# One more lane step in the memory attention of a hybrid encoder layer, and higher pacing rates for its lane in five stages

## Chip, cores and metric

The kernel runs on one core of one Trainium2 chip. The metric is the device time of one execution in microseconds; lower is better. The core has five engines with queues of their own, which work side by side: TensorE (PE; its weight loads are listed apart as PEld), VectorE (DVE), ScalarE (ACT), GpSimd (POOL) and SyncE (SP), whose queue issues nearly all DMAs here.

## What is computed

One layer of a bidirectional encoder with three parallel groups of heads, on two requests (256 and 1024 tokens, together 10 tiles of 128) with shared weights, in float32:

```python
hn = rms_norm(x, norm_g)
xbc, z_ssd, dt_raw, q, k, v, z_att, mq, z_mem = split_cols(hn @ w_in, IN_SIZES)
...                                                    # o_ssd: convolution, state scan both ways, gate, norm
...                                                    # o_att: windowed attention with 8 heads, gate
memn = rms_norm(mem, mem_norm_g)
mk, mv = split_cols(memn @ w_mem_kv, (MEM_WIDTH, MEM_WIDTH))      # 256 memory rows, 4 heads of 128
sm = einsum('bthd,bmhd->bhtm', rms_norm(mq), rms_norm(mk)) * MEM_HEAD_DIM ** -0.5
pm = softmax(sm, axis=-1)
o_mem = einsum('bhtm,bmhd->bthd', pm, mv) * silu(z_mem)
return x + concatenate([o_ssd, o_att, o_mem]) @ w_out
```

## The kernel before

Two kinds of work are woven together.

**The blocks** are the large products with `w_in`, `w_mem_kv` and `w_out`. A block takes its weights tile by tile over the inner dimension (16 tiles `k` of 128). Each weight tile is loaded by DMA into `wraw` and split by ScalarE and VectorE (L206, L207) into a high part `wh` and a low part `wl`; three matmuls then make one float32 product (L258 to L260 in `block_tok`, which makes rows of 5 token tiles at a time, 15 matmuls a tile `k`; L293 to L295 in `block_feat`). Blocks come in a fixed order. After the first half of the tokens (group 0) the second half (group 1) takes the stages `kv`, `q`, `za`, `z0`, `z1`, `mq`, `zm`; then come the output blocks: four token blocks (`o`) and eight others over the whole output.

**The lanes** hold everything that isn't a block: normalising keys (`k_prep`), windowed attention (`attn`), memory attention (`mem_attn`) in lane 0; the step sizes (`dt_prep`) and the state scan up and down (`ssd_up`, `ssd_down`) in lane 1. Each is a Python generator for one token tile `t`, and its code from one `yield` to the next is one *lane step*. Steps are traced between the matmuls of the blocks: after each tile `k` the block calls `pump`, which credits each lane with that stage's rate and runs as many steps of it as there are whole credits, in turn with the other lane:

```python
for i in range(2):
    owed[i] = owed[i] + rates[i] if lanes[i] else 0.0
while max(owed) >= 1:
    i = turn[0] ^ 1
    i = turn[0] = i if owed[i] >= 1 else i ^ 1
    owed[i] -= 1
    if lanes[i]:
        step(lanes[i])
```

`RATES[1]` holds the pair of rates of each stage of group 1, lane 0 first. `block_feat` stages (`x`, `za`, `zm`) have two blocks or more of 16 calls at half the rate. In a token block the matmuls of the last two tiles `k` stand together, and their two calls come behind them, next to each other. What is needed before it has been traced is forced by `need`; what the lanes still hold in the third output block is emptied in one go there, and the pool `mp` is closed.

A planner in the framework turns this trace into the engines' queues: it takes instructions by priority and by the times at which it expects their data, so their order on an engine is near the order of the trace but not the same. Semaphores keep what depends on each other in order.

`mem_attn` handles a token tile in two pairs of heads. Step by step: load the queries; squares and norms; queries split, gates `zm` loaded; an empty step; `scores(0)`; `scores(1)`; an empty step; `turn_(0)`; `turn_(1)`; `values(0)`; `values(1)` and the store. `scores` makes the scores of a pair (TensorE, L745 to L747, into `pms`), takes their maximum (VectorE, L749, L750), the exponential with its sum (ScalarE, L754), and scales by the reciprocal of the sum (VectorE, L756, L759, into `mpr`). `turn_` transposes the probabilities on TensorE (L767, into `pmt`) and copies them out on ScalarE (L771, `mpT`). `values` multiplies by the memory's values (L782) and the gate (L785, `moT`). Tiles t = 0 to 4 come up from the end of stage `x` on, in `kv` and `q`; t = 5 to 9 in the first two output blocks.

Of the other lines that the prediction names, L641 and L643 are scores of windowed attention and their maximum, L625 its turned queries; L868 and L889 belong to the scan upwards, L1045 and L1062 to the scan downwards; L1009 and L1011 turn a finished tile of it; L213 loads a weight tile.

Of the kernel before, what the change touches and what calls it, by code (L numbers as in the profile page):

```python
# [29 lines left out]
RBB = 4  # L30

RATES = ({'kv': (4.0, 1.0), 'z1': (2.2, 1.7)},
         {'kv': (1.4, 1.5), 'x': (2.1, 2.15), 'q': (2.2, 2.5), 'za': (2.1, 2.5), 'z0': (2.1, 2.5),
          'z1': (2.05, 2.55), 'mq': (1.95, 2.7), 'zm': (1.75, 2.75), 'o': (2.1, 2.4)})
FAR = 1e30

UNITS = (0, 8, 1, 9, 2, 10, 3, 11, 4, 12, 5, 13, 6, 7)
# [7 lines left out]
def hymba_encoder_kernel(  # L45
# [37 lines left out]
    def psum(name):  # L83
        return mix.tile([P, 512], F32, tag="mix", name=name)
# [37 lines left out]
    def rsqrt(dst, src, scale, n):  # L122
        G.tensor_scalar(out=dst, in0=src, scalar1=scale, scalar2=EPS, op0=ALU.mult, op1=ALU.add)
        G.tensor_tensor(out=dst, in0=dst, in1=mhalf[:, :n], op=ALU.pow)

    def hv(ap, n=8):
        return ap.rearrange("p (h d) -> p h d", h=n)
# [287 lines left out]
    def w2(name):  # L415
        return mp.tile([P, 512], F32, tag="wa", name=name, bufs=WA)
# [286 lines left out]
    def mem_attn(t):  # L703
        grp, ti = divmod(t, 5)
        tc_ = slice(ti * P, (ti + 1) * P)
        qr = mp.tile([P, 512], F32R, tag="wa", name="mq", bufs=WA)
        q = qr.bitcast(F32)
        if grp == 0:
            S.dma_start(hv(q, 4), mT_d[:, :, tc_])
        else:  # L710
            S.dma_start(q, mq_d[t])
        yield

        def turned():
            ps = psum("pmq")
            for h in range(4):
                T.transpose(ps[:, h * P:(h + 1) * P].bitcast(F32R), qr[:, h * P:(h + 1) * P], identr)
            return ps

        tok_ = turned() if grp == 0 else q  # L720
        sq = w2("sq")
        A.activation(sq, tok_, AF.Square)
        ss = sm.tile([P, 4], F32, tag="s4", name="mss", bufs=4)
        V.reduce_sum(out=ss, in_=hv(sq, 4), axis=AX.X)
        r = sm.tile([P, 4], F32, tag="s4", name="mr", bufs=4)
        rsqrt(r, ss, 1.0 / P, 4)
        yield
        feat_ = q if grp == 0 else turned()
        qh = mp.tile([P, 512], F32R, tag="qT", name="mqh", bufs=2)
        A.activation(qh, feat_, AF.Copy)  # L730
        ql = mp.tile([P, 512], F32R, tag="qT", name="mql", bufs=2)
        V.tensor_sub(ql, feat_, qh.bitcast(F32))
        z = w2("zm")
        S.dma_start(hv(z, 4), zT_d[1][grp][:, :, tc_])
        yield
        yield
        st_ = {}

        def scores(hp):
            ps = psum("pms")  # L740
            for j in range(2):
                h = 2 * hp + j
                c = slice(h * P, (h + 1) * P)
                o = ps[:, j * 256:(j + 1) * 256]
                T.matmul(o, qh[:, c], mkH[:, h, :], start=True, stop=False)  # L745
                T.matmul(o, qh[:, c], mkL[:, h, :], start=False, stop=False)
                T.matmul(o, ql[:, c], mkH[:, h, :], start=False, stop=True)  # L747
            m = sm.tile([P, 2], F32, tag="m2", name="mm", bufs=10)
            V.reduce_max(out=m, in_=hv(ps, 2), axis=AX.X)  # L749
            V.scalar_tensor_tensor(out=m, in0=m, scalar=-1.0, in1=r[:, 2 * hp:2 * hp + 2], op0=ALU.mult, op1=ALU.mult)  # L750
            pr = mp.tile([P, 512], F32, tag="lg", name="mpr", bufs=2)
            den = sm.tile([P, 2], F32, tag="m2", name="mden", bufs=10)
            for j in range(2):
                A.activation(pr[:, j * 256:(j + 1) * 256], ps[:, j * 256:(j + 1) * 256], AF.Exp,  # L754
                             scale=r[:, 2 * hp + j:2 * hp + j + 1], bias=m[:, j:j + 1], accum_out=den[:, j:j + 1])
            V.reciprocal(out=den, in_=den)  # L756
            for j in range(2):
                c = slice(j * 256, (j + 1) * 256)
                V.tensor_scalar(out=pr[:, c], in0=pr[:, c], scalar1=den[:, j:j + 1], scalar2=0.5,  # L759
                                op0=ALU.mult, op1=ALU.mult)  # L760
            st_[hp] = pr

        def turn_(hp):
            pr = st_[hp]
            pt = psum("pmt")
            for a in range(4):
                T.transpose(pt[:, a * P:(a + 1) * P], pr[:, a * P:(a + 1) * P], ident)  # L767
            if hp == 0:
                st_["pT"] = mp.tile([P, 2, 768], F32, tag="pT", name="mpT", bufs=1)
            pT = st_["pT"][:, hp, :512]  # L770
            A.activation(pT, pt, AF.Copy)  # L771
            st_[hp] = pT

        oT = w2("moT")

        def values(hp):
            pT = st_.pop(hp)
            po = psum("pmo")
            for j in range(2):
                h = 2 * hp + j  # L780
                for a in range(2):
                    T.matmul(po[:, j * P:(j + 1) * P], mv[:, a, h * P:(h + 1) * P],  # L782
                             pT[:, (2 * j + a) * P:(2 * j + a + 1) * P], start=(a == 0), stop=(a == 1))
            c = slice(hp * 256, (hp + 1) * 256)
            V.tensor_mul(oT[:, c], po[:, :256], z[:, c])  # L785

        scores(0)
        yield
        scores(1)
        yield  # L790
        yield
        turn_(0)
        yield
        turn_(1)
        yield
        values(0)
        yield
        values(1)
        S.dma_start(oT_d[1][grp][:, :, tc_], hv(oT, 4))
        yield  # L800
# [649 lines left out]
    def refill_o(grp, when):  # L1450
        def f(k):
            if k not in when:
                return []
            q = when[k]
            need((attn, mem_attn, ssd_down, ssd_down)[q], range(grp * 5, grp * 5 + 5))
            return [part(fill_direct, q, j, oT_d[q][grp][:, j, :],
                         gain=None if q < 2 else vec[:, R_SG + 4 * (q - 2) + j:R_SG + 4 * (q - 2) + j + 1])
                    for j in range(4)]
        return f
# [126 lines left out]
    def when_done(n, then):  # L1586
# [9 lines left out]
        return f  # L1596

    queue(0, mem_attn, range(5))
    run(block_tok(w_in_rows("z1"), 5, ev_gate(1, 0)), RATES[0]["z1"], refill_x(1),
        extra=when_done(1, lambda: queue(1, ssd_up, range(4))))  # L1600
# [25 lines left out]
    tok("mq", w_in_rows("mq"), ev_raw(mq_d, 5), grp=1)  # L1626
    gate("zm", 1, refill_o(0, {3: 0, 7: 1}))
    queue(0, mem_attn, range(5, 8))
    queue(0, mem_swap, [0])
    queue(0, mem_values, [1])  # L1630
# [97 lines left out]
```

## Time and profile before

| what | value |
|---|---|
| time, median of 3 runs | 1793.29 us (1792.8 to 1793.42) |
| the profiled execution | 1792.72 us, of which the span from first to last instruction is 1791.0 us |
| granted clock of TensorE | 1.000 |
| PE, DVE, ACT, POOL busy | 99%, 70%, 51%, 31% of the span |
| DMA | 301.12 MB, mean 168 GB/s |

Line numbers (L767) are those of the kernel before. In the profile's rows `pmt<-identr,mpr` reads: tile `pmt` is written from `identr` and `mpr`; `128x512 f32` is partitions by elements. In a timeline the first two columns are the start and the duration in us, and `[1.09 <-DVE mpr L759]` says that the engine stood idle for 1.09 us before the instruction until that other instruction had ended. In a list of waits the three numbers are total us, count and the longest. A table by windows shows the busy time of each engine in each stretch of the span, with the number of its instructions.

### The profile page before, as it was taken

What the parts mean: (1) busy time and instruction counts of PE and PEld (TensorE: products, weight loads), DVE (VectorE), ACT (ScalarE), POOL (GpSimd) and SP (SyncE); (2) the same over time, 40 slices, a digit from 0 to 9 for tenths busy, and PEclk for the clock granted to TensorE, in tenths of its full rate; (3) what the DMA queues carried; (4) which work ended last, traced back from release to release, by engine and by line L of the source; (5) the groups of instructions that cost most, each with busy time, mean ns of one, the idle gap of its engine ahead of it and who ended that gap; (6) DMA issues with size and microseconds to landing.
All of it is one profiled execution on the core that took longest, in us unless ns stands there. A gap on an engine that the chain in (4) does not pass through costs nothing.

```text
span 1791.0 us, 31429 instructions
## 1 busy us (share of the span) xinstructions
PE 1777.5 (99%) x10838; PEld 1605.0 (90%) x10838; DVE 1248.7 (70%) x2358; ACT 922.2 (51%) x2049; POOL 549.6 (31%) x900
## 2 busy tenths in 40 slices
PE   9999999999999999999999999999999999999999
PEld 7789999999998999999889977877988888899999
DVE  5595788888868877778766575557777644766665
ACT  6554555554434766656465565544447533543332
POOL 0105789998810101001001000000100000057775
PEclk9999999999999999999999999999999999999999
DMA  8653444445446644453635645557777754744442
GB/s 292 199 180 114 144 148 149 144 142 163 123 145 207 188 142 137 136 162 111 193 111 179 182 149 162 165 160 249 233 224 238 240 185 149 223 149 144 148 142 77
DMA packets 208207, 301.12 MB, mean 168 GB/s; under 512 B 19568, under 2 KB 86192, under 8 KB 208048
## 3 DMA queue, kind: packets, MB, share of 16 engines
q1 hardware_dynamic: 207904, 299.06, 54.3%
q8 instruction: 85, 1.39, 0.3%
q14 instruction: 74, 0.61, 0.1%
q10 hardware_dynamic: 144, 0.06, 0.0%
HBM read 236.36 MB, written 62.69 MB: 167 GB/s over the span
## 4 chain that ended last, share of the span: by engine, by line
PE 71%; issue 7%; POOL 7%; DVE 6%; DMA 6%; ACT 3%; SPq 0%; POOLq 0%; ACTq 0%; DVEq 0%
PE acc L258 8%; PE acc L260 8%; PE acc L259 8%; PE acc L293 5%; PE acc L1237 5%; PE acc L295 5%; PE acc L294 5%; PE acc L1235 5%; PE acc L1236 5%; POOL ws L1207 4%; PE accm L1236 2%; PE accm L1235 2%; PE accm L1237 2%; POOL wraw L1207 2%; PE po L673 1%
## 5 line engine op out<-in xcount | busy, mean ns | idle before, releaser
L207 DVE TENSOR_TENSOR wl<-wraw,wh 128x512 fp32r<-128x512 f32 (+1 forms) x480 | 345.3, 721 | 220.0 <-ACT wh L206 199.8
L206 ACT ACTIVATE wh<-wraw 128x512 fp32r<-128x512 f32 (+1 forms) x480 | 292.1, 613 | 305.8 <-PE acc L260 154.1
L258 PE MATMUL acc<-wh,xH 128*128 128x512 f32 (+1 forms) x1088 | 418.4, 385 | 0.5 <-ACT mkr L420 0.3
L260 PE MATMUL acc<-wh,xL 128*128 128x512 f32 (+1 forms) x1088 | 411.2, 378 | 0.0
L259 PE MATMUL acc<-wl,xH 128*128 128x512 f32 (+1 forms) x1088 | 410.4, 377 | 0.7 <-DVE wl L207 0.7
L258 PEld LDWEIGHTS acc<-wh,xH 128*128 128x128 f32 x1088 | 204.5, 188 | 38.7 <-issue 3.6
L259 PEld LDWEIGHTS acc<-wl,xH 128*128 128x128 f32 x1088 | 204.6, 188 | 38.2 <-DVE wl L207 3.3
L260 PEld LDWEIGHTS acc<-wh,xL 128*128 128x128 f32 x1088 | 204.4, 188 | 36.8 <-issue 0.6
L293 PE MATMUL acc<-xH,wh 128*128 128x320 f32 x640 | 202.9, 317 | 0.5 <-DVE zs L309 0.5
L206 ACT ACTIVATE sh<-ws 128x384 fp32r<-128x384 f32 x176 | 91.4, 523 | 214.0 <-POOL ws L1207 117.0
L294 PE MATMUL acc<-xL,wh 128*128 128x320 f32 x640 | 199.2, 311 | 0.0
L295 PE MATMUL acc<-xH,wl 128*128 128x320 f32 x640 | 198.3, 310 | 0.0
L207 DVE TENSOR_TENSOR sl<-ws,sh 128x384 fp32r<-128x384 f32 x176 | 124.1, 708 | 105.1 <-ACT sh L206 104.9
L1207 POOL TENSOR_TENSOR ws<-wraw 128x128 f32<-128x128 f32 x176 | 113.5, 645 | 204.5 <-DMA wraw<-in_w_in_pairs_dram 81.1
L635 POOL COPY lg<-nsink 128x2 f32<-128x2 f32 x40 | 16.4, 410 | 373.9 <-PE ppt L663 239.6
L293 PEld LDWEIGHTS acc<-xH,wh 128*128 128x128 f32 x640 | 120.3, 188 | 3.3 <-issue 2.2
L294 PEld LDWEIGHTS acc<-xL,wh 128*128 128x128 f32 x640 | 120.3, 188 | 2.0 <-issue 1.7
L295 PEld LDWEIGHTS acc<-xH,wl 128*128 128x128 f32 x640 | 120.2, 188 | 0.8 <-issue 0.7
L1207 POOL TENSOR_TENSOR ws<-wraw,ws 128x128 f32<-128x128 f32 x176 | 116.6, 662 | 13.8
L1207 POOL TENSOR_TENSOR wraw<-wraw 128x128 f32<-128x128 f32 x176 | 112.2, 638 | 13.7
L1207 POOL TENSOR_TENSOR ws<-ws,wraw 128x128 f32<-128x128 f32 x176 | 115.0, 653 | 0.0
L362 DVE SCALAR_TENSOR_TENSOR c<-u,vec,c 128x638 f32<-128x638 f32 (+1 forms) x96 | 89.7, 936 | 8.9 <-ACT c L357 8.6
(437 smaller groups left out, 3947.0 us busy)
## 6 DMA issues: line engine op xcount, KB each, us to landing
wraw<-in_w_in_laid_dram SPq DMA_DIRECT2D x176, 256.0 KB, 2.9
wraw<-in_w_in_pairs_dram SPq DMA_DIRECT2D x112, 256.0 KB, 2.7
wraw<-in_w_out_laid_dram SPq DMA_DIRECT2D x64, 256.0 KB, 3.0
wraw<-in_w_out_pairs_dram SPq DMA_DIRECT2D x64, 256.0 KB, 2.9
rf<-ac SPq DMA_DIRECT2D x40, 256.0 KB, 4.0
rb<-ac SPq DMA_DIRECT2D x40, 256.0 KB, 4.9
wraw<-in_w_mem_laid_dram SPq DMA_DIRECT2D x32, 256.0 KB, 4.8
xst<-in_x_sample_dram SPq DMA_DIRECT2D x20, 256.0 KB, 4.9
```

Source lines behind the costliest of these rows:

```text
L206: a = A.activation(h, raw, AF.Copy)
L207: b = V.tensor_sub(l, raw, h.bitcast(F32))
L258: T.matmul(ps[t][:, :n], sh, h[:, :n], start=(k_ == 0), stop=False)
L259: T.matmul(ps[t][:, :n], sh, l[:, :n], start=False, stop=False)
L260: T.matmul(ps[t][:, :n], sl, h[:, :n], start=False, stop=(k_ == KT - 1))
L293: T.matmul(o, sh, cur["H", q][:, m, c], start=(k == 0), stop=False)
L294: T.matmul(o, sh, cur["L", q][:, m, c], start=False, stop=False)
L295: T.matmul(o, sl, cur["H", q][:, m, c], start=False, stop=(k == KT - 1))
L1207: G.tensor_tensor(out=o, in0=x, in1=y, op=op)
L1235: T.matmul(ps[p], h, xh, start=(k_ == 0), stop=False)
L1236: T.matmul(ps[p], h, xl, start=False, stop=False)
L1237: T.matmul(ps[p], l, xh, start=False, stop=(k_ == 7))
```

## The change

`mem_attn` yields once more between `scores(1)` and `turn_(0)`: two empty steps lie there instead of one, and each of its ten runs takes 13 lane steps instead of 12. In group 1 the rate of lane 0 is raised in the stages `kv` (1.4 to 1.5), `q` (2.2 to 2.25), `za` (2.1 to 2.15), `z1` (2.05 to 2.1) and `mq` (1.95 to 2.0), and in the output stage `o` (2.1 to 2.15). Lane 1's rates, and the rates of `x`, `z0` and `zm`, are as before.

```diff
-         {'kv': (1.4, 1.5), 'x': (2.1, 2.15), 'q': (2.2, 2.5), 'za': (2.1, 2.5), 'z0': (2.1, 2.5),
-          'z1': (2.05, 2.55), 'mq': (1.95, 2.7), 'zm': (1.75, 2.75), 'o': (2.1, 2.4)})
+         {'kv': (1.5, 1.5), 'x': (2.1, 2.15), 'q': (2.25, 2.5), 'za': (2.15, 2.5), 'z0': (2.1, 2.5),
+          'z1': (2.1, 2.55), 'mq': (2.0, 2.7), 'zm': (1.75, 2.75), 'o': (2.15, 2.4)})
...
         scores(0)
         yield
         scores(1)
+        yield
         yield
         yield
         turn_(0)
```

## The prediction

> **What bounds the kernel now.** The page comes first: its engine shares.
>
> ```profile
> span 1791.0 us, 31429 instructions
> PE 1777.5 (99%) x10838; PEld 1605.0 (90%) x10838; DVE 1248.7 (70%) x2358; ACT 922.2 (51%) x2049; POOL 549.6 (31%) x900
> ```
>
> TensorE (PE) has an instruction in flight in 99% of the span; the other engines have room. So the time is TensorE's own work plus the moments in which it stands still, and those are 1791.0 − 1777.5 = 13.5 us in all. The change adds, removes and reshapes no matmul: it can only move waits. The question is therefore which of these 13.5 us lie where the change reaches. The table by windows says so; I cut the span at 820 us (where memory attention begins), at 1480 us (where its last block has ended) and at 1591 us (where the last output blocks begin).
>
> ```profile
> core 0: us, PE busy (x) PEld busy (x) DVE busy (x) ACT busy (x) POOL busy (x), PEclk, DMA share, GB/s
> 0.00:820.00 820.00, 815.40 (x5143) 761.29 (x5144) 618.80 (x1116) 442.54 (x948) 342.25 (x541) 1.00 0.52 160
> 820.00:1480.00 660.00, 654.68 (x3858) 556.43 (x3857) 431.14 (x925) 357.11 (x885) 56.12 (x97) 1.00 0.61 189
> 1480.00:1591.00 111.00, 111.00 (x503) 91.13 (x503) 69.66 (x120) 48.13 (x85) 11.11 (x23) 1.00 0.54 167
> 1591.00:1791.00 200.00, 196.37 (x1339) 196.11 (x1337) 129.06 (x200) 74.38 (x134) 140.13 (x240) 1.00 0.44 134
> ```
>
> Everything before 820 us runs at rates and with steps that the diff leaves alone, and after 1480 us memory attention is over. Between them TensorE idles 660 − 654.68 = 5.3 us. That is what the change can work on. The list of TensorE's waits in this stretch gives 4.7 us of it a name:
>
> ```profile
> engine line waited for: us in total, times, longest us
> PE pmt L767 <- DVE mpr L759: 2.0, 3, 1.1
> PE pyb L1062 <- ACT so L1011: 1.1, 1, 1.1
> PE psc L641 <- DVE nm L643: 0.9, 1, 0.9
> PE pd L1045 <- DVE nm L643: 0.3, 1, 0.3
> PE psc L641 <- ACT qT L625: 0.2, 1, 0.2
> PE pst L868 <- DVE fl L889: 0.2, 1, 0.2
> ```
>
> The largest row is exactly the place of the new step: the turn of the probabilities (L767) waits for VectorE's scaling of them (L759), 2.0 us over three waits. The other 2.7 us belong to window attention (L641) and to the state scan (L868, L1045, L1062).
>
> **What one such wait costs, and why it is there.** The timeline at the worst one, the second memory attention block (t = 1, in the kv stage):
>
> ```profile
> 847.70 0.28 PE L747 MATMUL pms<-mkH,mql 128*128 128x256 f32 x1
> 851.10 0.56 ACT L754 ACTIVATE mpr<-pms,mm,mr 128x256 f32<-128x256 f32 x1 [0.55 <-DVE mm L750]
> 852.35 0.29 PE L260 MATMUL acc<-wh,xL 128*128 128x288 f32 x1
> 852.48 0.29 PE L258 MATMUL acc<-wh,xH 128*128 128x288 f32 x1
> 853.37 0.61 DVE L759 TENSOR_SCALAR mpr<-mpr,mden 128x256 f32<-128x256 f32 x2
> 853.86 0.52 PE L767 MATMUL pmt<-identr,mpr 128*128 128x128 f32 x3 [1.09 <-DVE mpr L759]
> ```
>
> The first pair's scores leave TensorE at 847.98 and the scaled probabilities are there at 853.37 + 0.61 = 853.98: a chain of 6.0 us over VectorE and ScalarE. TensorE reaches the turn after about 5 us. Its matmuls here start 0.13 us apart (852.35, 852.48), but from 852.48 to 853.86 it is 1.38 us: the wait costs 1.25 us, 0.16 more than the 1.09 in brackets. I count from start to start below. The other waits at L767, in blocks t = 6 and t = 7 (output stage):
>
> ```profile
> 1370.35 0.28 PE L747 MATMUL pms<-mkH,mql 128*128 128x256 f32 x1
> 1370.47 0.39 PE L258 MATMUL acc<-wh,xH 128*128 128x512 f32 x1
> 1370.70 0.39 PE L259 MATMUL acc<-wl,xH 128*128 128x512 f32 x1
> 1374.12 0.39 PE L259 MATMUL acc<-wl,xH 128*128 128x512 f32 x1
> 1375.30 0.63 PE L767 MATMUL pmt<-identr,mpr 128*128 128x128 f32 x4 [0.79 <-DVE mpr L759]
> 1375.69 0.48 PE L260 MATMUL acc<-wh,xL 128*128 128x512 f32 x1
> 1376.31 0.63 PE L767 MATMUL pmt<-identr,mpr 128*128 128x128 f32 x4
> 1402.30 0.60 PE L767 MATMUL pmt<-identr,mpr 128*128 128x128 f32 x4
> 1405.93 0.39 PE L260 MATMUL acc<-wh,xL 128*128 128x512 f32 x1
> 1406.47 0.30 PE L767 MATMUL pmt<-identr,mpr 128*128 128x128 f32 x1 [0.15 <-DVE mpr L759]
> ```
>
> Start to start against the undisturbed 0.23 us (1370.47 to 1370.70): 1375.30 − 1374.12 − 0.23 = 0.95; 1376.31 − 1375.69 − 0.23 = 0.39; 1406.47 − 1405.93 − 0.23 = 0.31. With the 1.25 the four waits cost 2.9 us.
>
> **The new step, counted out.** Four stages by the same table (kv, q, z0, first output block; I read their bounds off the evacuations of the blocks):
>
> ```profile
> 820.00:868.00 48.00, 46.87 (x365) 45.10 (x365) 38.45 (x86) 34.27 (x93) 5.47 (x5) 1.00 0.55 160
> 868.00:945.00 77.00, 76.94 (x414) 64.21 (x411) 51.98 (x120) 42.57 (x110) 5.43 (x10) 1.00 0.49 147
> 1011.00:1089.00 78.00, 77.00 (x407) 61.95 (x406) 48.79 (x110) 45.12 (x113) 4.39 (x9) 1.00 0.50 153
> 1328.00:1402.00 74.00, 72.86 (x400) 60.63 (x399) 47.22 (x93) 42.14 (x100) 3.84 (x7) 1.00 0.76 236
> ```
>
> A memory attention block takes 12 lane steps now and 13 after. The step issues no instruction. It only sets the turn later, so I counted the steps of both lanes call by call, with the old rates and the new ones (a call of the pacing stands behind each input tile of a block, 16 to a block; the last two calls of a token block stand next to each other). What matters is how many calls lie between a block's scores and its turns:
> - t = 1: scores in calls 8 and 9 of kv, turns in 10 and 11; after, both turns in 11. The first turn moves by a call, and 48 us of kv over 16 calls is 3.0 us a call (820 to 868): more than the 1.25 missing. That wait goes.
> - t = 6: both scores in call 8 of the first output block, both turns in 9; after, in 10. 74 us (1328 to 1402) over 16 calls is 4.6 us, against 0.95 + 0.39. Both waits go.
> - t = 7: scores in 13 and 14, turns in 15. After, the lane is later by then: both scores in 14, both turns in call 0 of the next block. Between them lies the k = 0 group of that block, 15 matmuls, 3.4 us: the pattern that t = 6 has before. So a new wait may stand there. Its bounds: nothing (block t = 3 has the same pattern in the q stage, where TensorE idles for 0.06 us in all, 77.00 − 76.94), or t = 6's 1.34. I take 1.3, since it is the same stage and load.
> - The others have two calls or more, or the distance they had.
>
> Sum: − 2.9 + 1.3 = − 1.6 us.
>
> **The rates.** Five memory attention blocks add 5 steps before zm. The raised rates give back 16 × 0.1 in kv, 16 × 0.05 in q, 32 × 0.025 in za, 16 × 0.05 in z1 and in mq: 4.8 steps. Window attention t = 4 to 9 and the key preparation in front of it so start in the same call as before or up to three calls later (three only inside za), and the last one ends in the same call of zm. In the output stage 41 calls × 0.05 give 2.05 against 5 steps: the lane ends two calls later, with seven calls left before what remains of the lanes is emptied. Lane 1 keeps its rates and its calls. So no step is forced, and no pool closes later.
>
> What is queued with a step: each block's loads of its queries and gates and its store go to SP's queue, in front of weight loads.
>
> ```profile
> SPq L213 <- DVE moT L785: 18.5, 7, 5.1
> ```
>
> Weight loads already stand behind the block's last product for up to 5.1 us, and no wait of the weight matmuls is in TensorE's list for this stretch: the loads run ahead. I cost this at nothing; without that lead a late load would cost up to those 5.1 us. The two buffers of probabilities are held one step longer, and the next user comes at least five steps behind the turn: nothing.
>
> The other 2.7 us of listed waits are re-dealt, since attention shifts by up to a call (4.6 us in the output stage, 78 / 16 = 4.9 in z0) against the state scan. They can vanish (− 2.7, with 0.16 a wait − 3.5) or be joined by others; without a row that favours a side I take zero and keep both ends for the range.
>
> The profiled execution took 1792.72 us (span 1791.0 and 1.7 around it), 0.57 under the median 1793.29. After: 1791.1 by the profile, **1791.7** by the median. About 0.2% (3.6 us) is what a measurement of this kernel can tell from no change.
>
> The matmul row's 99% caps any gain at the 5.3 us. The Trainium skill (Perfetto Trace Analysis, "Identifying the Most-Contended Engine") calls matmul busy time no good measure of headroom and takes LDWEIGHTS busy time instead; by that, 820 to 1480 us would hold 660 − 556.43 = 104 us. The trace speaks against using it here: from 1480 to 1591 us TensorE never idles (111.00 of 111) and its loads are busy for 91.13, 82%, about the 84% of our stretch. So its result changes nothing in my sum.
>
> **The rivals.**
> 1. *The planner undoes it.* TensorE's order is not the program's order alone: in block t = 7 both turns come out of one call, yet stand at 1402.30 and 1406.47, with 15 matmuls between. If turns stand where the planner expects their data, a step changes little, and the waits stay: 1793.3. Against it: t = 1 and t = 6 stand one call behind their scores, as counted.
> 2. *The shift helps attention too.* The 3.5 us above go and the new wait of t = 7 does not come: 1791.7 − 4.8 = 1786.9; about half of it gives 1789. It is over 0.2% from 2.0 of these 4.8 on. For it: these waits are single accidents of place. Against it: all must fall well.
> 3. *Slower: attention and state scan collide.* Lane 0 is denser in q, za, z1 and mq while lane 1 stays. Both use VectorE and ScalarE in order, and TensorE's transposes and state products (L641, L1009, L1045, L1062) stand in its queue ahead of the weight matmuls. A call's shift may set one directly behind its producer, at the price of L1062's or L641's wait: 1.1 or 0.9, with 0.16 more each. It decides from + 3.6 + 1.6 = 5.2 us on, that is five new waits; five or six give 1797.5 to 1798.5. For it: six blocks of attention and ten of state work lie in reach, each with several such points. Against it: the stretch has only five such waits now.
>
> **How the numbers follow.** My forecast 0.36 and the planner 0.14 both lie within 0.2%: same 0.50. Rival 2: faster 0.24. Rival 3: slower 0.26. The likeliest case alone runs from 1790 (no new wait at t = 7) to 1794 (two new ones elsewhere). The range reaches from 1787.5, short of rival 2's end, to 1799, past six collisions.
>
> **What would show it.** Right: L767 has no wait in kv; one or two near the seam between the first two output blocks; TensorE's idle time from 820 to 1480 us falls to 3.5 to 4.5 us; TensorE's matmul count is the same. Wrong: L767 still waits 2 us (rival 1); new rows of L641, L1045, L1062 of over 1 us (rival 3); or a wait of weight matmuls on L207, which would mean that SP's or VectorE's queue lost its lead.

## The result and the profile after

The changed kernel takes 1787.56 us in the median of 8 runs (1785.61 to 1792.47); the kernel before took 1793.36 us in 8 runs of the same series (1791.55 to 1794.36). The ratio is 0.9971, 95% interval 0.9961 to 0.9981: faster by 0.29%, 5 to 6 us. A second series with the same program gave 0.9978 (0.9970 to 0.9987). The forecast of 1791.7 had the direction and less than half of the size. The time lies 0.06 us above the lower end of the range (1787.5), so that it fell inside was luck.

The profiled execution of the first series was the slowest of its 8 runs (1792.47 us, span 1790.8), so beside it I use a profile of the same program from the second series (first experiment below; line numbers as before the change). The kernel before has two profiles too, the second from the last experiment of the first series, which runs it once more. First the windows of the changed kernel, in the order first profile, second profile (columns as before):

```profile
0.00:100.00 100.00, 95.71 (x409) 77.17 (x410) 53.22 (x91) 57.75 (x112) 7.35 (x20) 1.00 0.74 236
820.00:1480.00 660.00, 655.36 (x3872) 558.60 (x3871) 429.62 (x928) 358.07 (x887) 53.00 (x97) 1.00 0.61 189
1011.00:1241.00 230.00, 230.00 (x1233) 183.81 (x1231) 138.89 (x320) 125.23 (x310) 18.60 (x39) 1.00 0.56 175
```
```profile
0.00:100.00 100.00, 96.78 (x412) 78.14 (x413) 54.46 (x92) 58.73 (x114) 6.80 (x20) 1.00 0.74 239
820.00:1480.00 660.00, 656.07 (x3871) 558.93 (x3871) 429.57 (x927) 357.94 (x887) 53.18 (x97) 1.00 0.61 190
1011.00:1241.00 230.00, 230.00 (x1238) 183.39 (x1236) 138.86 (x321) 125.55 (x311) 18.91 (x40) 1.00 0.56 175
```

And the kernel before over the stretch from z0 to mq, first profile and second:

```profile
1011.00:1241.00 230.00, 228.80 (x1222) 181.60 (x1222) 138.41 (x316) 123.21 (x306) 18.21 (x39) 1.00 0.56 172
```
```profile
820.00:1480.00 660.00, 654.54 (x3858) 555.96 (x3857) 431.45 (x925) 357.68 (x886) 56.10 (x97) 1.00 0.60 187
1011.00:1241.00 230.00, 229.55 (x1228) 182.66 (x1228) 140.08 (x319) 123.60 (x307) 18.18 (x39) 1.00 0.55 171
```

From 820 to 1480 us TensorE idles for 4.6 and 3.9 us instead of 5.3 and 5.5. From z0 to mq it no longer idles at all (1.2 and 0.45 us before). The idle in the first 100 us (4.3 and 3.2 us; 2.3 and 3.2 before) is not the change's: no instruction there is moved.

The idle column shows only part of what was gained. A better ruler is the time between two points which the change leaves in place: the last copy of the last x block (L394) and the last sum of the fourth output block (L410). First profile before, then the two of the changed kernel:

```profile
L394 ACT ACTIVATE u<-acc x12: 413/438/440, 617.9 to 820.3; 128x320 f32<-128x320 f32 x12
L326 ACT ACTIVATE qs<-acc x15: 577/588/599, 146.3 to 1241.1; 128x512 f32<-128x512 f32 x15
L410 DVE TENSOR_TENSOR yt<-acc,yt x20: 679/684/693, 1396.4 to 1590.8; 128x512 f32<-128x512 f32 x20
```
```profile
L394 ACT ACTIVATE u<-acc x12: 416/437/441, 620.0 to 822.0; 128x320 f32<-128x320 f32 x12
L326 ACT ACTIVATE qs<-acc x15: 577/586/601, 148.7 to 1241.2; 128x512 f32<-128x512 f32 x15
L410 DVE TENSOR_TENSOR yt<-acc,yt x20: 680/684/692, 1395.4 to 1590.7; 128x512 f32<-128x512 f32 x20
```
```profile
L394 ACT ACTIVATE u<-acc x12: 417/438/440, 618.2 to 820.3; 128x320 f32<-128x320 f32 x12
L326 ACT ACTIVATE qs<-acc x15: 576/589/601, 148.1 to 1239.2; 128x512 f32<-128x512 f32 x15
L410 DVE TENSOR_TENSOR yt<-acc,yt x20: 673/680/692, 1392.8 to 1588.0; 128x512 f32<-128x512 f32 x20
```

L394 to L410 is 1590.8 − 820.3 = 770.5 us before (771.7 in the second profile), 768.7 and 767.7 after: 2.9 us less in the mean. Cut at the end of mq (L326), about 1.5 us of it lie ahead of that point (420.8 and 420.2 before, 419.2 and 418.9 after) and about 1.5 behind it (349.7 and 351.5; 349.5 and 348.8). The first of these is clean: in three of the four profiles TensorE does 2457 weight loads between the two points, in the fourth 2458. The second lies within the 1.8 us by which the two profiles of the kernel before differ there. The busy time of the weight loads (LDWEIGHTS, the column PEld) over the fixed stretch of 660 us says the same of the whole: 556.4 and 556.0 us before, 558.6 and 558.9 after, that is 2.6 us more loads done in the same time, at 84% about 3 us of progress. The Trainium skill (Perfetto Trace Analysis, "Identifying the Most-Contended Engine") prefers LDWEIGHTS busy time, next to MFU (the share of the peak rate of operations that is reached), to matmul busy time for judging headroom. Here it served as a measure of progress, and agrees with the ruler. Between these 2.9 us and the 4 to 6 us of the timed runs lies what single profiles can't resolve: the part ahead of 820 us alone, which no kernel here changes, ended between 818.6 and 822.5 us in the profiles.

### The profile page after: what moved, and what is told of

It is laid out like the page before. It is cut to its first block, busy times and chain, and to the rows that moved or that the text cites. A ratio compares the mean times of both kernels' runs of the same rounds, so it can differ in the third digit from the quotient of the medians.

```text
span 1790.8 us, 31435 instructions
## 1 busy us (share of the span) xinstructions
PE 1776.3 (99%) x10838; PEld 1605.2 (90%) x10838; DVE 1246.8 (70%) x2358; ACT 921.7 (51%) x2049; POOL 549.3 (31%) x900
## 4 chain that ended last, share of the span: by engine, by line
PE 79%; issue 6%; POOL 5%; DMA 5%; DVE 3%; ACT 2%; SPq 0%; POOLq 0%; ACTq 0%; DVEq 0%
PE acc L258 9%; PE acc L260 9%; PE acc L259 9%; PE acc L1238 6%; PE acc L1236 6%; PE acc L1237 6%; PE acc L293 5%; PE acc L295 5%; PE acc L294 5%; POOL ws L1208 3%; PE accm L1237 2%; PE accm L1236 2%; PE accm L1238 2%; PE po L673 1%; PE ppt L663 1%
## 5 line engine op out<-in xcount | busy, mean ns | idle before, releaser
L258 PE MATMUL acc<-wh,xH 128*128 128x512 f32 (+1 forms) x1088 | 419.0, 385 | 2.7 <-ACT mkr L420 1.3
```

Of the source, the lines that this page charges most:

```text
L258: T.matmul(ps[t][:, :n], sh, h[:, :n], start=(k_ == 0), stop=False)
```

## Experiments

**First series: the whole once more, its two parts, and nothing.** My theory: the step takes the waits at L767 away and the rates only bring the lane back. Rivals: the rates make the gain; or it lies at the start and is not the change's.

The whole change, both yields on one line:

```diff
         scores(1)
-        yield
+        yield; yield
```


> The whole change once more, with both yields on one line so that line numbers stay. Theory A (the step takes the waits at L767 away and the shift happens to spare attention and the state scan others): ratio to the kernel before 0.996 to 0.998, TensorE idle from 820 to 1480 us at most 3.5 us instead of 5.3, and 4.6 us before 820 us as in the kernel before. Theory B (what was timed lies in the first 100 us, where loads from memory set the pace and which vary from run to run): ratio 0.998 to 1.000, idle from 820 to 1480 us between 4.5 and 5.5 us. Theory C (time is lost inside busy stretches, in matmuls that start late, and the idle column does not show it): ratio near 0.997 with idle of 4.5 us or more in that stretch.

Measured: 0.9978 (0.9970 to 0.9987), 1788.79 us. The start (rival B) falls: the idle ahead of 820 us is no smaller, the stretch behind it is shorter. A and C share the rest: idle is 3.9 us, between what A and C wrote, and the ruler finds more than the idle column. That the rest lies in matmuls which start late inside busy stretches is argued, not shown. The waits of TensorE from 820 to 1480 us:

```profile
PE pmt L767 <- DVE mpr L759: 1.4, 2, 1.3
PE pyb L1062 <- ACT so L1011: 1.1, 1, 1.1
PE pst L867 <- ACT fh L881: 0.6, 1, 0.6
PE pd L1045 <- DVE nm L643: 0.5, 1, 0.5
PE pst L868 <- DVE bl L910: 0.2, 1, 0.2
```

Window attention's waits (L641) are gone. L767 is not: 1.4 us instead of 2.0. And a wait has joined that neither profile of the kernel before has: in the first output block, just behind the turns of t = 5, the state scan waits for ScalarE (L867), here 0.6 us. In the first profile of the changed kernel it is longer (there the line is L868):

```profile
PE pst L868 <- ACT fh L882: 1.6, 1, 1.6
```

The timeline in kv, block t = 1 (the first row is the first pair's turn, the last the second pair's):

```profile
854.69 0.60 PE L767 MATMUL pmt<-identr,mpr 128*128 128x128 f32 x4
854.98 0.56 ACT L754 ACTIVATE mpr<-pms,mm,mr 128x256 f32<-128x256 f32 x1
856.08 0.62 DVE L759 TENSOR_SCALAR mpr<-mpr,mden 128x256 f32<-128x256 f32 x2
856.58 0.63 PE L767 MATMUL pmt<-identr,mpr 128*128 128x128 f32 x4 [1.29 <-DVE mpr L759]
```

The first pair no longer waits. But both turns now come out of one call, one behind the other, and the second pair's scaling is only then under way. Before, the first pair's wait had covered the second's. In t = 6 both pairs turn without a wait, four transposes and four:

```profile
1375.62 0.39 PE L260 MATMUL acc<-wh,xL 128*128 128x512 f32 x1
1375.86 1.03 PE L767 MATMUL pmt<-identr,mpr 128*128 128x128 f32 x8
1376.64 0.48 PE L258 MATMUL acc<-wh,xH 128*128 128x512 f32 x1
```

In t = 7, at the seam between the first two output blocks, the second pair waits 0.15 us:

```profile
1404.54 0.41 PE L767 MATMUL pmt<-identr,mpr 128*128 128x128 f32 x2 [0.15 <-DVE mpr L759]
```

The step alone, rates as before (`yield; yield`, nothing else):

> The extra step alone, the rates as before. Theory A: most of the gain stays, ratio 0.997 to 0.999, no wait at L767 in the kv stage. Rival (the rates make the gain, the step costs a delay that they make good): ratio 1.000 to 1.002, since lane 0 runs up to five steps late from kv to zm.

Measured: 0.9990 (0.9981 to 1.0000), 1791.39 us. Small, between the two expectations. kv loses its wait (TensorE 47.74 of 48 us), but a new one of 2.2 us stands at L767 in the output stage, behind ScalarE's exponential. Behind it TensorE runs at half its clock for a while: matmuls that stood 0.23 us apart stand 0.43 us apart, and the granted clock (the column PEclk, third from the right) is 0.51:

```profile
1348.26 0.66 PE L767 MATMUL pmt<-identr,mpr 128*128 128x128 f32 x4 [2.18 <-ACT mpr L754]
1350.62 0.63 PE L260 MATMUL acc<-wh,xL 128*128 128x512 f32 x1
1351.05 0.63 PE L258 MATMUL acc<-wh,xH 128*128 128x512 f32 x1
```
```profile
1349.00:1352.00 3.00, 3.00 (x9) 2.32 (x8) 3.00 (x9) 3.00 (x9) 0.00 (x0) 0.51 0.90 297
```

From 1348.99 to 1352.33 us there are eight steps from matmul to matmul, which at 0.23 us take 1.84: the stall costs about 1.5 us more than its own 2.2. The same is seen in three more profiles below, of the rates alone, of two extra steps and of the empty steps with the second half: one wait each of 2.30, 2.27 and 2.07 us, and a granted clock of 0.50 for two full microseconds after it. One wait of 2.17 us, in the profile of the rates alone, is not followed by a lower clock, and no profile whose longest wait is 1.6 us or less shows one. So in this profile the step alone lost nearly 4 us to one stall; five of its 12 runs show a mean granted clock under 1.000.

The rates alone:

```diff
-         {'kv': (1.4, 1.5), 'x': (2.1, 2.15), 'q': (2.2, 2.5), 'za': (2.1, 2.5), 'z0': (2.1, 2.5),
-          'z1': (2.05, 2.55), 'mq': (1.95, 2.7), 'zm': (1.75, 2.75), 'o': (2.1, 2.4)})
+         {'kv': (1.5, 1.5), 'x': (2.1, 2.15), 'q': (2.25, 2.5), 'za': (2.15, 2.5), 'z0': (2.1, 2.5),
+          'z1': (2.1, 2.55), 'mq': (2.0, 2.7), 'zm': (1.75, 2.75), 'o': (2.15, 2.4)})
```


> The five rates alone, 12 steps as before. Theory A: no gain, ratio 0.9995 to 1.002, and the waits at L767 total 2 us or more, since the turns stand nearer to the scores. Rival (the rates make the gain): ratio 0.997 to 0.998 with L767's waits unchanged at 2.0 us.

Measured: 1.0022 (1.0012 to 1.0032), 1796.30 us: slower. The rival falls, and the denser lane has a price of its own:

```profile
820.00:1480.00 660.00, 651.15 (x3823) 551.79 (x3823) 426.95 (x920) 355.26 (x882) 56.66 (x97) 1.00 0.60 186
```
```profile
PE pyf L884 <- DVE moT L785: 2.3, 1, 2.3
PE pmt L767 <- ACT rb L930: 2.2, 1, 2.2
PE pmt L767 <- DVE mpr L759: 1.6, 2, 1.4
PE pmq L717 <- DMA mq<-mT: 1.6, 1, 1.6
```

TensorE idles for 8.9 us instead of 5.3. L767 waits 3.8 us in all, and where steps lie nearer to each other even a load of queries is waited for (L717). The clock has its part too: nine of the 11 runs show a mean granted clock under 1.000, against two of 35 of the kernel before and none of the 19 of the changed kernel. The two runs at 1.000 took 1793.55 and 1795.08 us. So the parts don't add: − 0.10% and + 0.22%, together − 0.22 to − 0.29%. The rates need the step. Whether the step needs the rates is not shown, since the step alone met the stall above.

The kernel before once more (a comment added):

> The kernel before, once more as a kernel of its own. Every theory: ratio 1.000 within 0.0007; its profile shows how much of the waits before 820 us and after it differ from run to run of the same program (theory B: by over 2 us in the first 100 us; A: under 1 us).

Measured: 1.0000 (0.9990 to 1.0010), 1793.11 us, profile with a span of 1794.3. The interval is wider than I wrote. The first 100 us hold 0.9 us more idle than the first profile's, under what B needed, and L394 lies 2.2 us later.

**Second series: halves, kv, and a second step.** Theory now: a sum of local savings. Rival: an accident of one order, which needs the whole.

The first half: the step for t = 0 to 4, the rates of kv, q, za, z1 and mq, and o back at 2.1:

```diff
+        yield from (None,) * (2 if t < 5 else 1)
```


> The change in the first half alone: the extra step for t = 0 to 4 and the rates of kv, q, za, z1 and mq; the output stage (t = 5 to 9, rate o) as before. If the gain is a sum of local savings, as the profiles of the whole change say (about 1.8 us by start-to-start times from 945 to 1241 us, nothing in kv and q, 1.6 us from 1328 to 1480 us): ratio 0.9985 to 0.9995, TensorE idle under 0.3 us from 1011 to 1241 us and 1.1 us or more from 1328 to 1402 us. If the gain needs the whole (an accident of one order): 0.9995 to 1.001.

Measured: 0.9984 (0.9975 to 0.9994). The second half: the step for t = 5 to 9 and only the rate of o:

```diff
+        yield from (None,) * (2 if t >= 5 else 1)
```


> The change in the second half alone: the extra step for t = 5 to 9 and the rate of o; everything up to zm as before. Sum of local savings: ratio 0.9985 to 0.9997, waits at L767 from 1328 to 1480 us at most 0.3 us in all, those of kv (1.1 us) and the waits of window attention and state scan from 1011 to 1241 us (0.5 to 1.2 us) as before. Accident of one order: 0.9995 to 1.001.

Measured: 0.9988 (0.9979 to 0.9996). Both gain, and − 0.16% and − 0.12% make − 0.28%, the whole. The accident of one order falls for the first half; the interval of the second just reaches its lower end (0.9995). The profiles (the window from z0 to mq and the waits of the first half, then of the second):

```profile
1011.00:1241.00 230.00, 230.00 (x1239) 183.36 (x1238) 138.90 (x321) 125.57 (x310) 18.91 (x40) 1.00 0.57 175
```
```profile
PE pmt L767 <- DVE mpr L759: 2.1, 2, 1.3
```
```profile
1011.00:1241.00 230.00, 228.93 (x1224) 181.50 (x1224) 138.28 (x317) 123.09 (x306) 18.21 (x39) 1.00 0.56 171
```
```profile
PE pst L867 <- ACT fh L881: 1.3, 1, 1.3
PE pmt L767 <- DVE mpr L759: 1.1, 2, 0.9
PE psc L641 <- DVE nm L643: 0.8, 1, 0.8
```

The first half clears z0 to mq and leaves L767 at 2.1 us: it gains nothing there. By the ruler it takes 419.0 us to the end of mq, as the whole change. The second half halves L767 (what is left is kv's 0.9 and one short wait) and leaves z0 to mq as it was. But it brings the new wait at L867, 1.3 us, and its profile shows no gain: TensorE idles for 5.6 us from 820 to 1480 us, and the ruler gives 770.5 us, as in the first profile before. Its 0.12% rests on the timed runs alone.

The whole change with kv back at 1.4, q 2.3 and za 2.2:

> The whole change, but kv stays at 1.4 and q and za go to 2.3 and 2.2 instead of 2.25 and 2.15, so that window attention starts in the same calls as in the whole change. Both turns of t = 1 then come three calls after both scores. If the distance in calls decides: no wait at L767 in kv (the whole change has 1.1 to 1.3 us there), idle from 820 to 868 us under 0.8 us instead of 1.5, and 1.2 us less than the whole change, ratio 0.9965 to 0.9975. If a denser lane 0 in kv is what helps: 0.998 or more.

Measured: 0.9974 (0.9965 to 0.9982). As expected L767's wait in kv goes and kv idles for 0.5 us (47.53 of 48). The time can't be told from that of the whole change: 1.2 us are 0.07%, less than the 0.09% by which the interval reaches to either side. The ruler, one profile each, leans to it, 766.8 us against 768.7 and 767.7:

```profile
L394 ACT ACTIVATE u<-acc x12: 414/437/440, 615.4 to 818.6; 128x320 f32<-128x320 f32 x12
L410 DVE TENSOR_TENSOR yt<-acc,yt x20: 673/682/692, 1389.8 to 1585.4; 128x512 f32<-128x512 f32 x20
```

Part of what kv gains goes to the next product, which waits instead:

```profile
PE pmo L782 <- ACT mpT L771: 0.6, 1, 0.6
PE pmt L767 <- DVE mpr L759: 0.2, 1, 0.2
```

Two extra steps, rates raised twice as far:

> Two extra steps (14 lane steps), rates raised twice as far (kv 1.6, q 2.3, za 2.2, z1 2.15, mq 2.05, o 2.2). If the distance between scores and turn is what was missing, the waits at L767 are nearly gone after one step, so a second brings at most the 1.5 us that were left: ratio 0.9965 to 0.998, waits at L767 under 0.4 us. If the denser lane makes the gain, about twice that of the whole change: 0.993 to 0.996. If denser lanes cost and only the step hides it: 0.998 to 1.001 with new waits in other rows.

Measured: 0.9988 (0.9978 to 0.9999), so no more gain than from one step, and by the median less. L767 has no row left in the list of waits; others took its place (the first two rows):

```profile
PE pd L1045 <- DMA ydT<-yd: 2.3, 1, 2.3
PE pst L867 <- ACT fh L881: 1.2, 1, 1.2
```

That is the third expectation: once L767 waits no more, more distance saves nothing there, and new waits stand elsewhere. The 2.3 us wait is one of those with half the clock behind it. Whether the rates or the second step bring these waits is not told apart here.

**Third series: is the first half's gain lane 0's place?** After the five longer blocks, attention's t = 5 starts one call later in z0. So I moved it there without the change: two empty steps ahead of the key preparation of t = 5.

```diff
     def k_prep(t):
-        r = w2("kr")[:, :P]
+        yield from (None,) * (2 * (t == 5)); r = w2("kr")[:, :P]
```


> The kernel before, with its 12 steps and its rates, and two empty steps of lane 0 ahead of the key preparation of t = 5. Window attention of t = 4 to 7 then starts in the same calls as in the whole change; from t = 8 on it is one to two calls later than there. If it is lane 0's place against the state scan that saves the time from 945 to 1241 us: idle from 1011 to 1241 us under 0.4 us (1.2 and 0.5 us in the two profiles of the kernel before), ratio 0.998 to 0.9995, and kv and the output stage as before. If the denser rates of z1 and mq save it: idle there as before, ratio 0.9995 to 1.001.

Measured: 1.0002 (0.9993 to 1.0010), nothing gained. z0 does clear, but the lane, which nothing brings back, meets the state scan later (the same window, and the longest waits):

```profile
1011.00:1241.00 230.00, 229.04 (x1228) 182.60 (x1228) 137.01 (x316) 124.10 (x305) 17.87 (x39) 1.00 0.57 175
```
```profile
PE pyb L1062 <- DVE oT L676: 1.2, 1, 1.2
PE psc L641 <- ACT pT L664: 1.0, 1, 1.0
PE ppt L663 <- DVE lg L651: 0.8, 1, 0.8
```

The same with the second half of the change:

> The same two empty steps, and the change's second half: the extra step for t = 5 to 9 and the rate 2.15 in the output stage. The extra step for t = 0 to 4 and all other rates are left out. If the whole gain is place of lane 0 in z0 to mq, plus L767's waits in the output stage: ratio 0.997 to 0.9985, about the whole change. If the step in kv and q is needed: 0.9985 to 0.9997, that of the second half alone.

Measured: 0.9989 (0.9981 to 0.9998), the second half's own 0.9988. The empty steps add nothing to it either. Its profile, of the longest of the 12 runs, holds a wait of 2.1 us at L641 with half the clock behind it.

A version meant to be better than both, kv at 1.4, q at 2.25, za at 2.25:

> The whole change with kv at 1.4 and za at 2.25 (q at 2.25): the distance of three calls in kv that took L767's wait away there, attention in the same calls as in the whole change, and t = 2 to 4 half a call later than with q at 2.3. If the savings add: no L767 wait in kv, none at the values of t = 4, ratio 0.9965 to 0.9975. If the time saved in kv is lost to the next wait: 0.9975 to 0.998.

Measured: 0.9970 (0.9958 to 0.9982) in 5 runs. kv runs free (47.90 of 48 us), but L782 waits 1.2 us for ScalarE's copy in the q stage. By time it can't be told from the whole change. The ruler gives 766.9 us, as for the version above:

```profile
L394 ACT ACTIVATE u<-acc x12: 415/438/440, 618.0 to 820.9; 128x320 f32<-128x320 f32 x12
L410 DVE TENSOR_TENSOR yt<-acc,yt x20: 673/680/693, 1392.3 to 1587.8; 128x512 f32<-128x512 f32 x20
```

The last one adds the rates of z1 and mq to the empty steps (z1 2.1, mq 2.0), so that the lane is late in z0 and back by zm:

> The two empty steps ahead of the key preparation of t = 5, and the changed rates of z1 and mq alone. Memory attention keeps its 12 steps; kv, q, za and o keep their rates. Window attention then runs in the calls of the whole change, but for 9 of its steps. If the first half's gain is lane 0's place, later by one call in z0 and back by zm: ratio 0.998 to 0.9993, idle from 1011 to 1241 us under 0.3 us, and waits of L641 and L663 on window attention from 1230 to 1328 us gone (3.0 us with the empty steps alone); kv and the output stage as in the kernel before. If the first half's gain needs the step within memory attention: 0.9995 to 1.001.

Measured: 1.0010 (1.0002 to 1.0019). The waits of L641 are gone from the list, that of L663 shrinks to 0.5 us, and z0 to mq idles for 0.5 us, no less than in the second profile before and more than the 0.3 expected; there is no gain in time. The ruler takes 419.7 us to the end of mq, between the whole change (418.9 and 419.2) and the kernel before (420.2 and 420.8). The theory of place alone falls as an account of the time, though this version did not quite reach the place of the whole change.

## Why the prediction was right or wrong

- *The bound.* Right in kind: TensorE's matmuls are the same 10838, and only their order and waits between 820 and 1591 us changed. But I took 5.3 us of idle as all there was to win and idle as the measure. The timed runs gained 3.8 and 5.8 us. The ruler gained 2.9 us where the idle column lost about 1.1 (5.3 and 5.5 to 4.6 and 3.9).
- *"− 2.9 at L767"* was mis-sized, by a step left out. For t = 6 it was right: no wait. For t = 1 I looked at the first pair only and let "that wait" go; both turns came into one call, and the second pair waited 1.29 us in its stead. The sentence that L767 would have no wait in kv was wrong. TensorE's idle, forecast at 3.5 to 4.5 us, came to 4.6 and 3.9.
- *"+ 1.3 at the seam"* was wrong too, in the other direction: there t = 7 waits 0.15 us, as before. The two errors nearly cancel. With start-to-start times L767 costs 1.45 (856.58 − 854.69 less four transposes, 0.44) plus about 0.3 instead of 2.9: − 1.15 where the sum said − 1.6.
- *"The other waits are re-dealt, I take zero"* is the term that was missed. Window attention's waits vanished from z0 to mq in both profiles. This is the prediction's second rival ("the shift helps attention too"), by about half, as it was priced there; it had 0.24, and the same-as-before case 0.50. The likeliest case, 1790 to 1794, missed; the range held only because it reached into this rival.
- *"The rates bring the lane back"* was right for the calls, and too harmless: alone they cost 0.22%; TensorE's added idle lies in kv and the first two output blocks, where memory attention runs, and part of the loss goes with the lowered clock. The planner did not undo the step (rival 1): two kernels that differ by it alone stand at 1.0022 and 0.9978. Rival 3, new collisions, came true for the rates alone, for two steps and for the empty steps. Here it came true by one row, L867's 1.6 and 0.6 us, which is not among the rows that I named; against t = 6's saving of 1.34 it takes back part in one profile and all in the other.
- *What stays open.* In the output stage t = 6's waits go, and the timed runs of the second half gain 0.12%; but L867 waits instead and that kernel's profile doesn't show the gain, so its cause is not shown. The first half gains 0.16%, its profile puts that into z0 to mq, and yet no kernel that put attention into nearly the same calls without the step gained anything in time. Whether the step within kv and q has an effect of its own, or the order within a call decides, these runs don't tell. That kv's wait, removed in two versions, leaves the time where it was can't be said: the ruler of both is about 1.3 us shorter than that of the whole change, and the timed runs are too few to see it.

## What to carry to other kernels

With work woven in between matmuls, count for each producer and consumer how many slots lie between them, for every pair and not just the first, and compare with the chain's length: a slot more pays only where the chain was longer, and a wait removed for one pair can uncover the next. Try spacing and pace together: here the spacing alone looked like little and the pace alone like a loss, while together they gained. Look at the granted clock behind every long wait: of the five waits of over 2 us in these profiles four were followed by half the clock, at about 1.5 us more in the one worked out. To see gains of a few tenths of a per cent, measure between two fixed points on either side of the change, in several profiles, rather than by one span or by idle time.

## What the runs showed that I had not expected

The same program varies by several us from run to run on one core: the 35 runs of the kernel before in the first series lie between 1790.27 and 1796.78 us, though three earlier ones lay within 0.6 us. In the profiles much of it arises before 820 us, where x ends between 818.6 and 822.5 us. So an interval of ± 0.1% needs some ten runs here. A part of the spread goes with the clock: 14 of the 110 runs of the kernel before, over all experiments, show a mean granted clock of 0.999; the medians of these lie 4 us above the others' in the first and second series, and about 1 us in the last two sets of runs.

A wait of TensorE of just over 2 us was enough, in four cases of five, for its clock to be halved for 3 to 4 us afterwards.
